# A mixture of softmaxes on one core: a unit of work takes every second row of a block of 256

## Chip, cores, metric

One core of a Trainium2 chip, the other cores idle. The metric is the device time of one execution in microseconds (us), as a median of several executions. Names in capitals are the core's engines: DVE (VectorE), ACT (ScalarE), POOL (GpSimd), SP (the engine that here only issues transfers).

## The reference

```python
# logits: (32, 128, 4, 4096) float32; prior: (32, 128, 4) float32
prior_probs = softmax(prior, axis=-1)
mixture = sum over the 4 heads of prior_probs[..., None] * softmax(logits, axis=-1)
# result: (32, 128, 4096) float32
```

268.4 MB of logits are read and 67.1 MB of result are written. A row (one batch and sequence position) has 4 heads of 4,096 floats, 64 KB that lie together in memory; its result is 16 KB.

## The kernel before

A unit of work is one batch: 128 rows, one per partition. It has 32 units, two logits buffers of 64 KB per partition, two result buffers, and two buffers for exponentials. Cut to what matters:

```python
P = 128                                   # B, S, H, V = 32, 128, 4, 4096

def load(b, eng=nc.sync):                 # issued from SP
    lt = lpool.tile([P, H, V], FP32, name="ltile")          # 2 buffers
    n = pieces(b)                         # 1 head at a time for the first unit and the last three, else all 4
    for h in range(0, H, n):
        eng.dma_start(out=lt[:, h : h + n], in_=logits[b, :, h : h + n, :])
    ltiles[b] = lt

def store(b, lo=0, hi=V, eng=nc.sync):    # issued from ACT in mid-run
    eng.dma_start(out=out[b, :, lo:hi], in_=accs[b][:, lo:hi])

# the prior: 32 partitions (batches) x 128 positions x 4 heads, softmax over heads,
# then turned by four 32-row transposes into pp[position, head, batch]
# ...
for b in range(B):
    # ... result tile acc; the store of unit b-1 is issued here
    for h in range(H):
        et = ebuf[:, h % 2]               # the last two units work in place
        nc.scalar.activation(et, lt[:, h], AF.Exp, accum_out=dsum[:, col])
        nc.vector.reciprocal(rden[:, col], dsum[:, col])
        if h == 0:
            nc.vector.tensor_scalar(out=acc, in0=et, scalar1=rden[:, col],
                                    scalar2=pp[:, h, b : b + 1], op0=ALU.mult, op1=ALU.mult)
            continue
        nc.gpsimd.tensor_mul(coeff[:, col], rden[:, col], pp[:, h, b : b + 1])
        nc.vector.scalar_tensor_tensor(out=acc, in0=et, scalar=coeff[:, col], in1=acc,
                                       op0=ALU.mult, op1=ALU.add)      # cut: the last head in two halves
    if b + 2 < B:
        load(b + 2)                       # waits until unit b has been read out of its buffer
```

The softmax here doesn't subtract the row's maximum and nothing guards it: scores larger than these inputs give would overflow.

## Time and profile before

| | before |
|---|---|
| time, median | 783.3 us (783.27 to 783.39, 6 runs) |
| span of the profiled run | 781.3 us |
| DVE busy, ACT busy | 68%, 60% |
| packets of the two data queues, share of 16 DMA engines' span | 82.1% + 17.6% |
| rate in mid-run | 433 GB/s |

The first lines are from the page of the kernel before: the span, the two data queues (packets, MB, share of the 16 DMA engines' time), the chain of waits that ended last (by engine and by line), and two groups of instructions (busy time, mean of one in ns, idle time before them and what ended most of it).

```profile
span 781.3 us, 851 instructions
...
q1 hardware_dynamic: 7056, 276.83, 82.1%
q10 hardware_dynamic: 4080, 58.79, 17.6%
...
DMA 66%; ACT 14%; DVE 10%; issue 7%; SPq 0%; POOL 0%; DVEq 0%; POOLq 0%; ACTq 0%
DMA ltile<-in_logits_dram 66%; ACT ebuf L107 14%; DVE acc L128 9%; DVE ltile L128 1%; SPq L43 0%; POOL coeff L123 0%; DVE rden L116 0%; DVEq L166 0%; DVE ltile L118 0%; POOLq L166 0%; ACTq L107 0%
...
L107 ACT ACTIVATE ebuf<-ltile 128x4096 f32<-128x4096 f32 x120 | 433.0, 3609 | 284.5 <-DMA ltile<-in_logits_dram 241.0
L116 DVE RECIPROCAL rden<-dsum 128x1 f32<-128x1 f32 x128 | 20.4, 160 | 206.3 <-ACT ebuf L107 206.3
...
```

The two queues together keep 16 DMA engines busy for 99.7% of the span. ACT and DVE have idle time, and what ends it is the arrival of logits (241.0 us on ACT) or the exponentials that follow from it (206.3 us on DVE). The chain of waits is two thirds logits loads.

The next lines are windows of the same trace: from and to, the length, the busy time of each engine, the granted clock, the share of the 16 DMA engines that was busy, and the rate in GB/s. Later windows are shown without the heading; their columns are these.

```profile
core 0: us, DVE busy (x) ACT busy (x) POOL busy (x), PEclk, DMA share, GB/s
100.00:200.00 100.00, 68.48 (x33) 60.68 (x34) 2.30 (x12) 1.00 1.00 433
200.00:300.00 100.00, 68.37 (x35) 61.27 (x33) 2.49 (x13) 1.00 1.00 433
300.00:400.00 100.00, 67.93 (x35) 59.38 (x34) 2.49 (x13) 1.00 1.00 433
```

Share 1.00 with 433 GB/s is 27.1 GB/s for each busy engine. Reading a rate and a share together is what most of this document does: a full share says only that packets were in flight, and the rate beside it says how long each took (a share of 0.99 went with only 278 GB/s in move_sbuf, experiment 4).

The trace also has a record of each DMA packet, with its size and duration. A logits row is one packet of 65,536 bytes in mid-run. The least of the 3,584 durations of such packets is 2,418 ns, and so are the median and the 95th percentile. A 16 KB packet takes 611 ns, whether it loads from HBM or stores to HBM. I call the time above these minimums (and those of the few smaller packets), summed over all packets of the two data queues and divided by 16 engines, the *slow-packet time* of a run: 2.2 us in the kernel before. The sum of the minimum times is 777.2 us per engine. The rest of the span, after a sixteenth of the time of all packets is taken off, is the time in which an engine had no packet: 1.7 us.

Last, the start of the run in order of time (start, duration, engine, line, operation; in brackets the idle time before and what ended it):

```profile
5.80 0.67 DVE L58 TENSOR_REDUCE pmax<-pr 32x128 f32<-32x512 f32 x1 [5.80 <-DMA pr<-in_prior_dram]
...
10.65 1.25 DVE L75 STREAM_TRANSPOSE pp<-pn 32x128 f32<-32x128 f32 x4
...
12.81 2.41 DVE L118 TENSOR_SCALAR acc<-ebuf,rden,pp 128x4096 f32<-128x4096 f32 x1
...
17.97 4.49 DVE L128 SCALAR_TENSOR_TENSOR acc<-ebuf,coeff,acc 128x4096 f32<-128x4096 f32 x1 [0.31 <-POOL coeff L123]
...
32.35 0.37 ACTq L49 DMA_DIRECT2D out_dram<-acc  x1
45.37 3.62 ACT L107 ACTIVATE ebuf<-ltile 128x4096 f32<-128x4096 f32 x1 [18.04 <-DMA ltile<-in_logits_dram]
```

The prior is ready at 11.9 us (last transpose), the first unit's first DVE pass starts at 12.81, its result is stored from 32.35 on, and load 1 has arrived at 45.37.

### The profile page before, as it was taken

How to read it: one execution, taken by the hardware profiler on the slowest of the kernel's cores; microseconds unless marked ns; L12 is line 12 of the kernel's file. 1: busy time of each engine (PE TensorE's matmuls, PEld its weight loads, DVE VectorE, ACT ScalarE, POOL GpSimd, SP SyncE). 2: the span in 40 equal slices, each digit the busy share in tenths (PEclk: the TensorE clock that was granted, in tenths of full speed). 3: DMA queues.
4: the chain of work that ended last, by engine and by line, in shares of the span. 5: the costliest groups of instructions: out<-in, count | busy, mean ns of one | idle time of the engine just before them, and what ended most of it. 6: DMA issues, size and time to landing. Idle time of an engine off the chain costs nothing.

```text
span 781.3 us, 851 instructions
## 1 busy us (share of the span) xinstructions
DVE 527.9 (68%) x266; ACT 470.0 (60%) x258; POOL 18.6 (2%) x100
## 2 busy tenths in 40 slices
DVE  4647677666786666865668666677666776668994
ACT  5366556755567555575555765547655577558971
POOL 0000000000000000000000000000000000000000
DMA  9999999999999999999999999999999999999998
GB/s 373 448 416 440 434 416 456 410 463 405 460 409 456 416 443 429 419 454 415 458 408 450 419 464 406 456 427 430 432 430 439 426 446 412 457 408 430 429 429 364
DMA packets 11143, 335.67 MB, mean 430 GB/s; under 512 B 1248, under 2 KB 1248, under 8 KB 1280
## 3 DMA queue, kind: packets, MB, share of 16 engines
q1 hardware_dynamic: 7056, 276.83, 82.1%
q10 hardware_dynamic: 4080, 58.79, 17.6%
q14 instruction: 7, 0.06, 0.0%
HBM read 268.50 MB, written 67.11 MB: 430 GB/s over the span
## 4 chain that ended last, share of the span: by engine, by line
DMA 66%; ACT 14%; DVE 10%; issue 7%; SPq 0%; POOL 0%; DVEq 0%; POOLq 0%; ACTq 0%
DMA ltile<-in_logits_dram 66%; ACT ebuf L107 14%; DVE acc L128 9%; DVE ltile L128 1%; SPq L43 0%; POOL coeff L123 0%; DVE rden L116 0%; DVEq L166 0%; DVE ltile L118 0%; POOLq L166 0%; ACTq L107 0%
## 5 line engine op out<-in xcount | busy, mean ns | idle before, releaser
L107 ACT ACTIVATE ebuf<-ltile 128x4096 f32<-128x4096 f32 x120 | 433.0, 3609 | 284.5 <-DMA ltile<-in_logits_dram 241.0
L128 DVE SCALAR_TENSOR_TENSOR acc<-ebuf,coeff,acc 128x4096 f32<-128x4096 f32 x90 | 403.6, 4484 | 27.4 <-POOL coeff L123 27.4
L116 DVE RECIPROCAL rden<-dsum 128x1 f32<-128x1 f32 x128 | 20.4, 160 | 206.3 <-ACT ebuf L107 206.3
L118 DVE TENSOR_SCALAR acc<-ebuf,rden,pp 128x4096 f32<-128x4096 f32 x30 | 72.4, 2412 | 1.3 <-DVE rden L116 0.3
L123 POOL TENSOR_TENSOR coeff<-rden,pp 128x1 f32<-128x1 f32 x96 | 18.4, 191 | 748.1 <-DVE rden L116 748.1
L107 ACT ACTIVATE ltile<-ltile 128x4096 f32<-128x4096 f32 x8 | 28.9, 3608 | 4.3 <-DMA ltile<-in_logits_dram 4.3
L128 DVE SCALAR_TENSOR_TENSOR ltile<-ltile,coeff 128x4096 f32<-128x4096 f32 (+1 forms) x7 | 27.0, 3874 | 1.8 <-POOL coeff L123 1.8
L107 ACT ACTIVATION_READ_ACCUMULATOR ebuf<-ltile 128x1 f32 x120 | 22.4, 187 | 0.0
L118 DVE TENSOR_SCALAR ltile<-ltile,rden,pp 128x4096 f32<-128x4096 f32 x2 | 4.8, 2412 | 0.1
L58 DVE TENSOR_REDUCE pmax<-pr 32x128 f32<-32x512 f32 x1 | 0.7, 674 | 5.8 <-DMA pr<-in_prior_dram 5.8
L62 ACT ACTIVATE pe<-pc 32x512 f32<-32x512 f32 x1 | 0.6, 628 | 4.8 <-DVE pc L60 4.8
L62 ACT ACT_TABLE_LOAD x1 | 1.3, 1283 | 1.2 <-PEq L155 1.2
L107 ACT ACTIVATION_READ_ACCUMULATOR ltile<-ltile 128x1 f32 x8 | 1.5, 186 | 0.0
L75 DVE STREAM_TRANSPOSE pp<-pn 32x128 f32<-32x128 f32 x4 | 1.2, 302 | 0.1
L64 DVE TENSOR_REDUCE psum<-pe 32x128 f32<-32x512 f32 x1 | 0.7, 674 | 0.7 <-ACT pe L62 0.7
L69 DVE TENSOR_TENSOR pn<-pe,prec 32x512 f32<-32x512 f32 x1 | 1.0, 1042 | 0.0
L66 DVE RECIPROCAL prec<-psum 32x128 f32<-32x128 f32 x1 | 0.9, 941 | 0.0
L60 DVE TENSOR_TENSOR pc<-pr,pmax 32x512 f32<-32x512 f32 x1 | 0.7, 680 | 0.0
L155 POOL MEMSET const-float32-0.0<- 128x1 f32 x1 | 0.1, 99 | 0.2 <-issue 0.2
L155 POOL MEMSET const-bfloat16-1.0<- 128x1 bf16 x1 | 0.1, 102 | 0.0
L155 POOL MEMSET const-uint8-127<- 128x1 uint8 x1 | 0.1, 102 | 0.0
L155 POOL MEMSET const-float32-1.0<- 128x1 f32 x1 | 0.1, 99 | 0.0
## 6 DMA issues: line engine op xcount, KB each, us to landing
out_dram<-acc ACTq DMA_DIRECT2D x28, 2048.0 KB, 29.3
ltile<-in_logits_dram SPq DMA_DIRECT2D x16, 2048.0 KB, 20.5
out_dram<-acc SPq DMA_DIRECT2D x2, 2048.0 KB, 32.9
out_dram<-ltile SPq DMA_DIRECT2D x1, 2048.0 KB, 21.2
out_dram<-ltile SPq DMA_DIRECT2D x2, 1024.0 KB, 8.7
ltile<-in_logits_dram SPq DMA_DIRECT2D x28, 32.3
pr<-in_prior_dram ACTq DMA_DIRECT2D x1, 64.0 KB, 5.0
```

The source lines that it names most:

```text
L58: nc.vector.reduce_max(pmax, pr, axis=AX.X)
L60: nc.vector.tensor_sub(pc, pr, pmax.unsqueeze(2).to_broadcast([B, S, H]))
L62: nc.scalar.activation(pe, pc, AF.Exp)
L64: nc.vector.reduce_sum(psum, pe, axis=AX.X)
L66: nc.vector.reciprocal(prec, psum)
L69: nc.vector.tensor_mul(pn.rearrange("b h s -> b s h"), pe, prec.unsqueeze(2).to_broadcast([B, S, H]))
L75: nc.vector.transpose(pp[32 * t : 32 * (t + 1)], pn[:, :, 32 * t : 32 * (t + 1)])
L107: ex = nc.scalar.activation(et, lt[:, h], AF.Exp, accum_out=dsum[:, col])
L116: nc.vector.reciprocal(rden[:, col], dsum[:, col])
L118: nc.vector.tensor_scalar(out=acc, in0=et, scalar1=rden[:, col], scalar2=pp[:, h, b : b + 1], op0=ALU.mult, op1=ALU.mult,)
L123: nc.gpsimd.tensor_mul(coeff[:, col], rden[:, col], pp[:, h, b : b + 1])
L128: nc.vector.scalar_tensor_tensor(out=acc[:, cs], in0=et[:, cs], scalar=coeff[:, col], in1=acc[:, cs], op0=ALU.mult, op1=ALU.add,)
```

## The change

A unit takes every second row of a block of 256 rows. The two units of a block read the even and the odd rows. What it was meant to gain is presumably better service from HBM. The prior's softmax has to follow the new order and works on 16 partitions of 256 positions instead of 32 of 128.

```diff
-    assert S == P and B == 32
+    J = 2
+    R = P * J
+    G = B * S // R
+    B = G * J
+    lg = logits.rearrange("b s h v -> (b s) h v").rearrange("(g p j) h v -> g j p h v", p=P, j=J)
+    ov = out.rearrange("b s v -> (b s) v").rearrange("(g p j) v -> g j p v", p=P, j=J)
+    pv = prior.rearrange("b s h -> (b s) h").rearrange("(g r) h -> g r h", r=R)
 # load and store:
-            eng.dma_start(out=lt[:, h : h + n], in_=logits[b, :, h : h + n, :])
+            eng.dma_start(out=lt[:, h : h + n], in_=lg[b // J, b % J, :, h : h + n, :])
-        eng.dma_start(out=out[b, :, lo:hi], in_=accs[b][:, lo:hi])
+        eng.dma_start(out=ov[b // J, b % J, :, lo:hi], in_=accs[b][:, lo:hi])
 # the prior (cut: softmax now in place, in pr and pmax):
-    pr = cpool.tile([B, S, H], FP32, name="pr")
+    pr = cpool.tile([G, R, H], FP32, name="pr")
+    pn = cpool.tile([32, H, R], FP32, name="pn")
+    nc.gpsimd.memset(pn, 0.0)
+    pq = pn.rearrange("g h (p j) -> g j h p", j=J)
-    pp = cpool.tile([P, H, B], FP32, name="pp")
-    for t in range(S // 32):
-        nc.vector.transpose(pp[32 * t : 32 * (t + 1)], pn[:, :, 32 * t : 32 * (t + 1)])
+    pp = cpool.tile([P, J, H, 32], FP32, name="pp")
+    for t in range(P // 32):
+        nc.vector.transpose(pp[32 * t : 32 * (t + 1)], pq[:, :, :, 32 * t : 32 * (t + 1)])
 # and pp[:, h, b : b + 1] becomes pp[:, b % J, h, b // J : b // J + 1]
```

By *pitch* I mean the distance in HBM between the rows of neighbouring partitions. The change doubles it: 128 KB instead of 64 KB for reads, 32 KB instead of 16 KB for writes.

More of the change, by code (lines that the diff above doesn't have):

```diff
@@ L26 @@
     P = 128
-    assert S == P and B == 32
+    J = 2
+    R = P * J
+    G = B * S // R
+    B = G * J
+    assert G * R == B * S and G <= 32
+    lg = logits.rearrange("b s h v -> (b s) h v").rearrange("(g p j) h v -> g j p h v", p=P, j=J)
+    ov = out.rearrange("b s v -> (b s) v").rearrange("(g p j) v -> g j p v", p=P, j=J)
+    pv = prior.rearrange("b s h -> (b s) h").rearrange("(g r) h -> g r h", r=R)
     lpool = ctx.enter_context(tc.tile_pool(name="lpool", bufs=2))
@@ L48, in store @@
     def store(b, lo=0, hi=V, eng=nc.sync):
-        eng.dma_start(out=out[b, :, lo:hi], in_=accs[b][:, lo:hi])
+        eng.dma_start(out=ov[b // J, b % J, :, lo:hi], in_=accs[b][:, lo:hi])
     load(0, eng=nc.sync)
-    pr = cpool.tile([B, S, H], FP32, name="pr")
-    nc.scalar.dma_start(out=pr, in_=prior)
+    pr = cpool.tile([G, R, H], FP32, name="pr")
+    nc.scalar.dma_start(out=pr, in_=pv)
     load(1, eng=nc.sync)
-    pmax = cpool.tile([B, S], FP32, name="pmax")
+    pn = cpool.tile([32, H, R], FP32, name="pn")
+    nc.gpsimd.memset(pn, 0.0)
+    pmax = cpool.tile([G, R], FP32, name="pmax")
     nc.vector.reduce_max(pmax, pr, axis=AX.X)
-    pc = cpool.tile([B, S, H], FP32, name="pc")
-    nc.vector.tensor_sub(pc, pr, pmax.unsqueeze(2).to_broadcast([B, S, H]))
-    pe = cpool.tile([B, S, H], FP32, name="pe")
-    nc.scalar.activation(pe, pc, AF.Exp)
-    psum = cpool.tile([B, S], FP32, name="psum")
-    nc.vector.reduce_sum(psum, pe, axis=AX.X)
-    prec = cpool.tile([B, S], FP32, name="prec")
-    nc.vector.reciprocal(prec, psum)
-    pn = cpool.tile([B, H, S], FP32, name="pn")
+    nc.vector.tensor_sub(pr, pr, pmax.unsqueeze(2).to_broadcast([G, R, H]))
+    nc.scalar.activation(pr, pr, AF.Exp)
+    nc.vector.reduce_sum(pmax, pr, axis=AX.X)
+    nc.vector.reciprocal(pmax, pmax)
     nc.vector.tensor_mul(
-        pn.rearrange("b h s -> b s h"), pe, prec.unsqueeze(2).to_broadcast([B, S, H])
+        pn[0:G].rearrange("g h r -> g r h"), pr, pmax.unsqueeze(2).to_broadcast([G, R, H])
     )
-    pp = cpool.tile([P, H, B], FP32, name="pp")
-    for t in range(S // 32):
-        nc.vector.transpose(
-            pp[32 * t : 32 * (t + 1)], pn[:, :, 32 * t : 32 * (t + 1)]
-        )
+    pq = pn.rearrange("g h (p j) -> g j h p", j=J)
+    pp = cpool.tile([P, J, H, 32], FP32, name="pp")
+    for t in range(P // 32):
+        nc.vector.transpose(pp[32 * t : 32 * (t + 1)], pq[:, :, :, 32 * t : 32 * (t + 1)])
     NCHUNK = 2
@@ L118 @@
                 nc.vector.tensor_scalar(
-                    out=acc, in0=et, scalar1=rden[:, col], scalar2=pp[:, h, b : b + 1],
+                    out=acc, in0=et, scalar1=rden[:, col], scalar2=pp[:, b % J, h, b // J : b // J + 1],
                     op0=ALU.mult, op1=ALU.mult,
@@ L122 @@
                 continue
-            nc.gpsimd.tensor_mul(coeff[:, col], rden[:, col], pp[:, h, b : b + 1])
+            nc.gpsimd.tensor_mul(coeff[:, col], rden[:, col], pp[:, b % J, h, b // J : b // J + 1])
             n = NCHUNK if split else 1
```

## The prediction

> **What bounds the kernel now.** The DMA engines, at their own rate. The queue table gives 82.1% + 17.6% = 99.7% of 16 engines' span to the two data queues. DVE is 68% busy and ACT 60%. In steady state (windows of one pair of units, 100 to 293 us) a unit of 10.49 MB takes 24.15 us: 434 GB/s, DMA share 1.00. The chain of waits repeats: 32.3 us of a logits load, two softmax heads, one DVE pass, the next load. ACT idles for loads 241 us over 32 waits.
>
> The DMA records show what limits that rate. A logits row moves as one 65,536-byte packet, and from the 5th to the 95th percentile it takes exactly 2,418 ns: 27.1 GB/s per engine, 434 GB/s for 16. A 16 KB store packet takes 611 ns. Packets that took longer than this minimum add up to 2.2 us per engine over the whole run, 1.8 us of it in the first 80 us. So the distance between their reads isn't what holds the engines. [...]
>
> **What the change does.** Bytes, transfers and the order on their queues stay: a row is still 64 KB contiguous. Only addresses change: partition p takes row 2p+j, so read pitch goes from 64 to 128 KB and write pitch from 16 to 32 KB.
>
> The prior's preparation now works on 16 partitions with twice the elements in each. From today's times (674 + 680 + 628 + 674 + 941 + 1042 + 4 x 302 ns, about 6 us) I estimate 10 to 12 us; a POOL fill runs beside the prior's load. It starts when the prior lands (5.8 us) and so ends near 17 us instead of 11.9; the first DVE pass then starts 4 to 5 us later than 12.8 us. Waits absorb most of it, so the first unit's last pass ends 1 to 2 us late, at about 34 us. Load 1 is in flight until 45 us, so the engines stay fed: off the critical path.
>
> **Worth.** At the packet minimum the transfers need 777 us per engine of a span of 781.3 us. All that a better address pattern could remove is the 2.2 us of slow packets, 0.3%. A gain of 2% (16 us) isn't there. A loss is possible if the new pitch makes engines collide in HBM. [...]
>
> **Predicted:** 783.4 us, 8 times in 10 between 781.0 and 788.0. Faster by over 2%: 0.01; within 2%: 0.93; slower by over 2%: 0.06.
>
> **What would show it.** Right: median 64 KB packet still 2,418 ns, DMA share 1.00 and 434 GB/s in mid-run windows, a unit every 24.15 us, the chain still two thirds logits loads; DVE prior operations about twice as long; the second load lands near 45 us. Wrong: packets longer than 2,418 ns[...], or shorter (then it was the reads and not the engines that set 2,418 ns); or an engine gap near 30 us because the first unit frees its buffer late.
>
> **What would make it wrong.** That 2,418 ns is an HBM figure of the 64 KB pitch and not the engine's own; [...] or that the head's slow packets grow.

The sum came to 783.4 us, the time before (783.3 us) with nothing taken away and nothing added: 777 us of packets at their minimum, 2.2 us of slow packets and about 2 us of other time make the span of 781.3 us. That engines might collide in HBM is a guess.

## The result

| | before | after |
|---|---|---|
| time, median (6 runs each) | 783.33 us | 783.49 us |
| range | 783.27 to 783.39 | 783.32 to 783.61 |
| 64 KB packet, median and 95th percentile | 2,418 and 2,418 ns | 2,418 and 2,418 ns |
| slow-packet time per engine | 2.2 us | 1.9 us |

The ratio of after to before is 1.0002, with a 95% interval from 0.9989 to 1.0015. Here and below a ratio is the mean time of one kernel's fast runs over that of the other's fast runs of the same rounds, so it is not quite the ratio of the medians. The result is correct. The time did not move.

The page after:

```profile
span 781.4 us, 853 instructions
...
q1 hardware_dynamic: 7056, 276.83, 82.1%
q10 hardware_dynamic: 4064, 58.79, 17.6%
...
DMA 66%; ACT 14%; DVE 10%; issue 7%; SPq 0%; POOL 0%; DVEq 0%; POOLq 0%; ACTq 0%
DMA ltile<-in_logits_dram 66%; ACT ebuf L110 14%; DVE acc L131 9%; DVE ltile L131 1%; SPq L51 0%; POOL coeff L126 0%; DVE rden L119 0%; DVEq L169 0%; DVE ltile L121 0%; POOLq L169 0%; ACTq L110 0%
...
L110 ACT ACTIVATE ebuf<-ltile 128x4096 f32<-128x4096 f32 x120 | 433.0, 3609 | 284.1 <-DMA ltile<-in_logits_dram 240.5
L119 DVE RECIPROCAL rden<-dsum 128x1 f32<-128x1 f32 x128 | 20.4, 159 | 203.8 <-ACT ebuf L110 203.8
...
```

The shares of the queues and of the chain are the same, and so are ACT's waits for logits (240.5 us against 241.0). The windows after:

```profile
100.00:200.00 100.00, 67.94 (x33) 60.16 (x34) 2.28 (x12) 1.00 1.00 433
200.00:300.00 100.00, 68.41 (x35) 61.30 (x33) 2.46 (x13) 1.00 1.00 433
300.00:400.00 100.00, 68.36 (x35) 59.35 (x34) 2.46 (x13) 1.00 1.00 433
```

And the start:

```profile
4.84 1.21 DVE L68 TENSOR_REDUCE pmax<-pr 16x256 f32<-16x1024 f32 x1 [4.84 <-DMA pr<-in_prior_dram]
...
13.45 1.78 DVE L80 STREAM_TRANSPOSE pp<-pn 32x256 f32<-32x256 f32 x4
15.27 2.41 DVE L121 TENSOR_SCALAR acc<-ebuf,rden,pp 128x4096 f32<-128x4096 f32 x1
...
18.06 4.49 DVE L131 SCALAR_TENSOR_TENSOR acc<-ebuf,coeff,acc 128x4096 f32<-128x4096 f32 x1 [0.31 <-POOL coeff L126]
...
32.30 0.37 ACTq L57 DMA_DIRECT2D out_dram<-acc  x1
44.84 3.62 ACT L110 ACTIVATE ebuf<-ltile 128x4096 f32<-128x4096 f32 x1 [17.87 <-DMA ltile<-in_logits_dram]
```

The prior's preparation got longer: 10.4 us (4.84 to 15.23) against 6.1 us (5.80 to 11.90). The prior landed 1.0 us earlier, so the first DVE pass is 2.5 us late (15.27 against 12.81). Already at the second pass only 0.1 us of that is left, because DVE had been idle for about 2.6 us between the two in the kernel before. The first store leaves at 32.30, earlier than before by 0.05 us.

### The profile page after: what moved, and what is told of

Same layout as the page of the kernel before. It is cut to its first block, busy times and chain, and to the rows that moved or that the text cites. A ratio compares the mean times of both kernels' runs of the same rounds, so it can differ in the third digit from the quotient of the medians.

```text
span 781.4 us, 853 instructions
## 1 busy us (share of the span) xinstructions
DVE 531.3 (68%) x266; ACT 470.4 (60%) x258; POOL 19.3 (2%) x101
## 3 DMA queue, kind: packets, MB, share of 16 engines
q10 hardware_dynamic: 4064, 58.79, 17.6%
## 4 chain that ended last, share of the span: by engine, by line
DMA 66%; ACT 14%; DVE 10%; issue 7%; SPq 0%; POOL 0%; DVEq 0%; POOLq 0%; ACTq 0%
DMA ltile<-in_logits_dram 66%; ACT ebuf L110 14%; DVE acc L131 9%; DVE ltile L131 1%; SPq L51 0%; POOL coeff L126 0%; DVE rden L119 0%; DVEq L169 0%; DVE ltile L121 0%; POOLq L169 0%; ACTq L110 0%
## 5 line engine op out<-in xcount | busy, mean ns | idle before, releaser
L110 ACT ACTIVATE ebuf<-ltile 128x4096 f32<-128x4096 f32 x120 | 433.0, 3609 | 284.1 <-DMA ltile<-in_logits_dram 240.5
L68 DVE TENSOR_REDUCE pmax<-pr 16x256 f32<-16x1024 f32 x1 | 1.2, 1207 | 4.8 <-DMA pr<-in_prior_dram 4.8
L73 DVE TENSOR_TENSOR pn<-pr,pmax 16x1024 f32<-16x1024 f32 x1 | 1.9, 1906 | 0.1
L71 DVE TENSOR_REDUCE pmax<-pr 16x256 f32<-16x1024 f32 x1 | 1.2, 1207 | 1.1 <-ACT pr L70 1.1
L80 DVE STREAM_TRANSPOSE pp<-pn 32x256 f32<-32x256 f32 x4 | 1.7, 434 | 0.1
L72 DVE RECIPROCAL pmax<-pmax 16x256 f32<-16x256 f32 x1 | 1.7, 1741 | 0.0
```

The source lines that it names most:

```text
L68: nc.vector.reduce_max(pmax, pr, axis=AX.X)
L71: nc.vector.reduce_sum(pmax, pr, axis=AX.X)
L72: nc.vector.reciprocal(pmax, pmax)
L73: nc.vector.tensor_mul(pn[0:G].rearrange("g h r -> g r h"), pr, pmax.unsqueeze(2).to_broadcast([G, R, H]))
L80: nc.vector.transpose(pp[32 * t : 32 * (t + 1)], pq[:, :, :, 32 * t : 32 * (t + 1)])
L110: ex = nc.scalar.activation(et, lt[:, h], AF.Exp, accum_out=dsum[:, col])
```

## The experiments

The result agrees with the prediction, so the question is whether it does for the stated reason. The theories:

- **A**: each DMA engine, or the way through which it alone reaches memory, moves 27.1 GB/s and no more. HBM has enough left, so addresses don't matter; the prior's preparation is hidden.
- **B**: the new pitch did gain something, and the heavier preparation of the prior took it back.
- **C**: HBM, or something else that all engines share, gives 434 GB/s in all, at either pitch.

There are 12 runs, in three groups on a chip each, all timed in 3 rounds beside the kernel before. Kernels that move data only, or mix up rows, give a wrong result.

### 1. The change without its addresses: rows_in_order

```diff
 # in the changed kernel
-    lg = ....rearrange("(g p j) h v -> g j p h v", p=P, j=J)
+    lg = ....rearrange("(g j p) h v -> g j p h v", p=P, j=J)      # out and pq likewise
```

> The changed kernel with everything of the change but its addresses: a unit takes 128 rows in order again (pitch 64 KB), while the prior keeps its 16-partition preparation. Theory A (the engines' own rate binds, the rest is hidden): 783.4 us, within 0.2% of before; 64 KB packets at 2,418 ns; load 1 lands near 45 us. Theory B (the pitch gained something and the heavier preparation ate it up, so that the sum is zero): slower than before by the preparation's cost, 2 to 4 us (0.3 to 0.5%). Theory C (HBM binds, at the same rate in both patterns): 783.4 us as well; this run does not tell A from C.

Measured: correct, 783.53 us against 783.29, ratio 1.0003 (0.9986 to 1.0020). Load 1 was there at 44.76 us.

### 2. The addresses alone: addresses_only

```diff
 # in the kernel before
-            eng.dma_start(out=lt[:, h : h + n], in_=logits[b, :, h : h + n, :])
+            eng.dma_start(out=lt[:, h : h + n], in_=lg[b // J, b % J, :, h : h + n, :])   # J = 2; stores likewise
```

> The kernel before with only the addresses of loads and stores changed (every second row of 256); the prior stays as before, so the coefficients belong to other rows and the result is wrong on purpose. Theory A: 783.4 us, within 0.2% of before, 64 KB packets at 2,418 ns. Theory B: faster than before by 2 to 4 us (0.3 to 0.5%). Theory C: 783.4 us.

Measured: wrong, 783.30 us against 783.29, ratio 1.0000 (0.9985 to 1.0015); slow-packet time 1.8 us. With run 1 this settles B: each half of the change by itself leaves the time as it was, within 0.2%. There were not two effects that cancelled.

### 3. Larger pitches: pitch_2mb, pitch_512k, addr_pitch_2mb, addr_pitch_512k

The first two take every 32nd or every 8th row, load the prior in that layout (`pr[p, g, j, h]`, no transposes) and give the right result. The last two are addresses_only with another J:

```diff
-    J = 2
+    J = 32        # or 8
```

> Each partition takes every 32nd row: read pitch 2 MB, write pitch 512 KB, 64 KB rows; the prior is loaded in that layout, no transposes; right result. Theory A: as long as HBM keeps up, 783.4 us and 2,418 ns; if this pitch, 16 times that of the change, makes engines collide, packets get longer and the time grows in proportion[...]. Theory C (HBM binds already at 64 KB pitch): packets change with the pitch at once, also at 128 KB, so a longer packet here and none at 128 KB speaks against it.

> As pitch_2mb, but every 8th row of 1024: read pitch 512 KB, write pitch 128 KB; right result. It asks where between 128 KB and 2 MB the packets begin to grow. [...] 783.4 us within 0.3%, under 3 us of slow packets per engine. If the loss grows with the pitch instead of setting in late: 786 to 795 us.

> addresses_only with every 8th row of 1024 (read pitch 512 KB, write pitch 128 KB) and the prior as before, so the result is wrong on purpose. pitch_512k changed the prior's load too (it landed at 22.8 us instead of 5.8) and scattered from 785 to 807 us; this run has the pitch alone. If the pitch does it: 785 to 807 us again and 64 KB packets over 2,418 ns. If the late prior did it: 783.4 us within 0.2%.

> addresses_only with every 32nd row (read pitch 2 MB, write pitch 512 KB), the prior as before, wrong on purpose. If the pitch cost pitch_2mb its 3.5%: 806 to 815 us again, slow packets of about 20 us per engine, nearly all of them loads. If its other prior did: 783.4 us.

| run | read pitch | time, median | before, same rounds | ratio (95% interval) | slow-packet time |
|---|---|---|---|---|---|
| before | 64 KB | 783.3 us | | | 2.2 us |
| addresses_only | 128 KB | 783.30 us | 783.29 us | 1.0000 (0.9985 to 1.0015) | 1.8 us |
| addr_pitch_512k | 512 KB | 786.08 us | 783.40 us | 1.0039 (1.0024 to 1.0054) | 3.6 us |
| addr_pitch_2mb | 2 MB | 807.62 us | 783.40 us | 1.0314 (1.0287 to 1.0340) | 19.7 us |
| pitch_512k | 512 KB | 785.5 and 787.3 us (fast), 801.7 and 807.4 us (slow) | 783.33 us | 1.0040 (1.0020 to 1.0060), fast runs | 3.6 us |
| pitch_2mb | 2 MB | 810.71 us | 783.29 us | 1.0354 (1.0322 to 1.0386) | 21.9 us |

So distance can matter, and the kernel before was not at a point where it does. The windows of addr_pitch_2mb:

```profile
0.00:50.00 50.00, 21.74 (x17) 16.76 (x10) 0.78 (x7) 1.00 0.95 372
100.00:200.00 100.00, 65.36 (x32) 58.91 (x33) 2.30 (x12) 1.00 1.00 426
200.00:300.00 100.00, 65.38 (x33) 59.53 (x35) 2.30 (x12) 1.00 1.00 426
760.00:803.00 43.00, 28.62 (x14) 19.51 (x12) 0.96 (x5) 1.00 0.88 360
```

In mid-run the engines are as busy as ever (share 1.00), but the rate is 426 instead of 433 GB/s: some packets are longer. Most 64 KB packets still take the minimum: the median is 2,418 ns as before, the upper quartile 2,493 ns and the 95th percentile 2,744 ns; one in three took over 2,425 ns. The stores of mid-run, at 512 KB pitch, stay fast: their packets add less than 0.1 us to the slow-packet time. The sum agrees with the time: 17.6 us more slow-packet time than before, and 4.6 us more in which an engine had no packet (6.3 us against 1.7), most of it at the end, where the engines finish apart. That makes 22.2 us, and the span grew by 22.2 us (803.5 against 781.3).

One expectation was off: the fast runs of pitch_512k lie 0.4% above the kernel before, with 3.6 us of slow packets, just over the 0.3% and 3 us expected. That engines collide in HBM at a large pitch is not shown; the longer packets and the lower rate are.

pitch_512k was a flawed experiment. Its prior came in 512 packets of 128 bytes between the logits and landed at 22.8 us, so more than the pitch had changed. Two of its four runs count as slow; the runs of the kernel before between them did not vary. With the pitch alone, addr_pitch_512k stays between 785.87 and 787.89 us. What made those two runs slow was not followed up.

C is hurt here but not dead. If HBM set the pace at 64 KB, I would expect any change of pattern to show (an assumption, not shown), and 64 to 128 KB does not (783.30 us against 783.29). But a shared limit outside HBM's addresses would look the same.

### 4. Logits out of SBUF: move_sbuf

Movement only: the 32 loads copy from a constant tile in SBUF, in the same packets.

```diff
-            eng.dma_start(out=lt[:, h : h + n], in_=logits[b, :, h : h + n, :])
+            eng.dma_start(out=lt[:, h : h + n], in_=src[:, h : h + n])
```

> Movement only: no softmax, the 32 loads of 8.39 MB come out of SBUF instead of HBM in the same packets (64 KB and 16 KB), the 32 stores of 2.1 MB go to HBM as before; the result is wrong on purpose. Theory A: 64 KB packets at 2,418 ns again, the same 27.1 GB/s without HBM on the read side, so about 777 us of packets per engine and 780 to 790 us in all, the fill of the source tile at the start included. Theory C (HBM reads set 2,418 ns): packets clearly other than 2,418 ns, shorter if SBUF answers faster. A third possibility, D: [...] packets become longer, which would leave A against C open.

Measured: 1,158 us, 64 KB packets of 3,522 to 4,066 ns, median 3,771.

```profile
100.00:500.00 400.00, 0.00 (x0) 1.78 (x9) 0.00 (x0) 1.00 1.00 325
500.00:1100.00 600.00, 0.00 (x0) 3.75 (x19) 0.00 (x0) 1.00 0.99 278
```

All engines are busy, at 278 GB/s in the second stretch. This is possibility D of the expectation: without HBM on the read side packets got longer, not shorter (3,771 ns in the median against 2,418). So a packet that stays within SBUF can be the slower one, but A and C are not told apart.

### 5. Movement without compute: move_all

Loads and stores of the kernel before and no softmax; stores send a constant tile. Two more things differ: the prior is not loaded, and every store leaves from ACT as soon as its unit's load has landed.

> Movement only, 64 KB pitch: the loads, packets and queues of the kernel before, but no softmax; the stores send a constant tile, so the result is wrong on purpose. Theory A (the engines' rate binds, compute is hidden): 778 to 785 us, as long as with the compute. Rival (the third of the chain of waits that is ACT and DVE is really paid): clearly shorter, by up to a quarter.

Measured: 791.5 us against 783.3, ratio 1.0106 (1.0091 to 1.0121). That is outside what theory A expected, on the side nobody expected: without any compute it is slower. The rival, that ACT's and DVE's third of the chain is paid, is refuted. The excess is in two places (the last line is the end of the kernel before):

```profile
20.00:100.00 80.00, 0.00 (x0) 0.59 (x3) 0.00 (x0) 1.00 1.02 437
200.00:300.00 100.00, 0.00 (x0) 0.59 (x3) 0.00 (x0) 1.00 1.02 435
770.00:789.00 19.00, 0.00 (x0) 0.20 (x1) 0.00 (x0) 1.00 0.65 276
...
770.00:781.00 11.00, 1.54 (x1) 0.00 (x0) 0.00 (x0) 1.00 0.78 332
```

With nothing to pace them, the stores pile up behind the loads (65 us from issue to landing in the median, against 29 us before), and at the end the engines finish unevenly: the last 19 us have a share of 0.65. Per engine, 6.3 us without a packet against 1.7, and 6.2 us of slow packets against 2.2: 8.6 us together, and the span grew by 8.3 (the prior's packets are missing here). Since the order of the stores changed too, this run alone is no exact bound. But in the kernel before an engine has no packet for only 1.7 us, so a faster ACT or DVE could bring back that much at most. It also shows that 777.2 us of packets per engine is a floor which not every order of issue comes close to.

### 6. Fewer engines: move_11_engines, ports_apart, ports_shared

move_11_engines is move_all on 88 of the 128 rows:

```diff
-            eng.dma_start(out=lt[:, h : h + n], in_=lg[b // J, b % J, :, h : h + n, :])
+            eng.dma_start(out=lt[0:88, h : h + n], in_=lg[b // J, b % J, 0:88, h : h + n, :])   # stores likewise
```

> As move_all, but every load and store takes 88 of the 128 rows. [...] So 11/16 of the bytes on 11/16 of the engines. Theory A (27.1 GB/s is each engine's own): packets stay at 2,418 ns, the time stays that of move_all within 1%, the rate falls to about 298 GB/s. Theory C (HBM or another shared resource gives 434 GB/s in all): packets shrink to about 2,418 x 11/16 = 1,660 ns and the time to about 540 us. The result is wrong on purpose.

Measured: 1,326 us; 64 KB packets of 4,794 ns in the median, 5,459 at most.

```profile
100.00:500.00 400.00, 0.00 (x0) 1.58 (x8) 0.00 (x0) 1.00 0.69 203
500.00:1200.00 700.00, 0.00 (x0) 3.36 (x17) 0.00 (x0) 1.00 0.69 151
```

A share of 0.69 is 11 of 16 engines busy on average, for 88 of 128 rows. But neither theory gave packets of about twice the length, and 31% fewer bytes than move_all took 68% more time. What I had not thought of is that it may matter which partitions of SBUF are written at the same time. The next two kernels test this alone. Each load is four transfers of 8 rows, the windows of both show a share of 0.49 to 0.52, which is 8 of 16 engines busy on average, and both kernels read the same rows from HBM:

```diff
 # ports_apart                                      # ports_shared
     for c in range(4):
-        ... out=lt[c : 32 : 4], in_=rows c : 32 : 4
+        ... out=lt[8 * c : 8 * c + 8], in_=rows c : 32 : 4
```

> Movement only, a quarter of the rows (32 of 128 of each unit) and one store at the end; wrong on purpose. Each load is four transfers of 8 rows[...]; here a transfer writes every fourth SBUF partition of 0 to 31[...]. Theory A1[...]: packets 2,418 ns, 217 GB/s, about 310 us in all. Theory A2 (the DMA engine itself moves 27.1 GB/s): the same. Theory C (HBM gives 434 GB/s in all): packets well under 2,418 ns, down to 1,209.

> As ports_apart, with the same rows read from HBM by the same number of engines, but each transfer writes 8 neighbouring partitions[...]. A2 (engine): 2,418 ns and about 310 us, as ports_apart. C: as ports_apart.

A1 is that SBUF's side of a transfer sets the pace, in a way that depends on which partitions are written together; A2 is the engine itself.

In both kernels the one store was issued at 5.16 us and not at the end, so in both it ran beside the first loads.

ports_apart: 323.0 us (322.93 to 323.08; about 310 were expected), 64 KB packets of 2,418 ns in the median, 2,458 at the 95th percentile.

```profile
20.00:70.00 50.00, 0.00 (x0) 0.98 (x5) 0.00 (x0) 1.00 0.50 215
120.00:170.00 50.00, 0.00 (x0) 0.99 (x5) 0.00 (x0) 1.00 0.51 220
220.00:270.00 50.00, 0.00 (x0) 0.99 (x5) 0.00 (x0) 1.00 0.49 212
```

Half the engines busy, about half the rate, the same packet. This is what refutes C: whatever all engines share was asked for 215 GB/s instead of 433, and packets did not get shorter (2,418 ns in the median). 27.1 GB/s belongs to the single engine, its way into SBUF, or its own way to HBM.

ports_shared: 452 to 503 us in four runs; three of them lie over 1.5% above the fastest and so count as slow, at the same granted clock, so only its packets and its distance from ports_apart (about 40% at the least) are used. The windows are of the profiled run, one of the slow ones (484.69 us):

```profile
20.00:70.00 50.00, 0.00 (x0) 1.68 (x3) 0.00 (x0) 1.00 0.52 95
120.00:170.00 50.00, 0.00 (x0) 0.59 (x3) 0.00 (x0) 1.00 0.50 136
220.00:270.00 50.00, 0.00 (x0) 0.59 (x3) 0.00 (x0) 1.00 0.50 127
370.00:420.00 50.00, 0.00 (x0) 0.99 (x5) 0.00 (x0) 1.00 0.51 206
```

The share is the same and the rate is not: 95 GB/s at first, up to 206 later. The first 16 packets took 7.5 to 9.1 us, 3.1 to 3.8 times the 2,418 ns of ports_apart. Over the whole run the median was 3,008 ns. A2 alone, which gave 2,418 ns, does not account for that, so A1 is possible. That writing to neighbouring partitions lengthens packets is shown; why it does, and why packets got shorter again in the course of the run, is not. Whether this explains the doubling in move_11_engines is open: only 5 of its 2,464 packets of 64 KB took under 2,500 ns, so all 11 engines were slowed, and how the rows were dealt to them was not looked at. Nor can these runs say whether, where nothing lengthens packets, it is the engine (A2), its way into SBUF (A1) or its own way to HBM that sets 2,418 ns: no run varied one of these alone and got shorter packets, and move_sbuf, which could have excluded HBM, had longer packets (3,771 ns) instead.

### 7. How much delay the start hides: slack_30

```diff
+    for _ in range(16):
+        nc.vector.tensor_mul(pn[0:G].rearrange("g h r -> g r h"), pr, pmax...)    # 1.9 us each
     nc.vector.tensor_mul(pn[0:G].rearrange("g h r -> g r h"), pr, pmax...)
```

> The changed kernel with the last operation of the prior's preparation done 16 more times, 1.9 us each: 30.5 us of delay before the first DVE pass, right result. Theory A, with the slack that I read: the first unit hides about 13 us of delay (load 2 may be issued at any time until load 1's packets end near 43 us; today it is issued near 28 us). With 30.5 us I expect load 2 to be issued near 57 us, a gap in the DMA of 13 to 16 us, and 796 to 800 us in all. If nothing of it were hidden: 814 us; if all of it: 783.5 us.

Measured: correct, 801.04 us against 783.33, ratio 1.0227 (1.0210 to 1.0244). The windows, then the lines that explain them:

```profile
20.00:40.00 20.00, 19.66 (x12) 0.00 (x0) 0.00 (x0) 1.00 1.08 466
42.00:57.00 15.00, 14.44 (x10) 7.42 (x4) 0.38 (x2) 1.00 0.00 0
100.00:200.00 100.00, 68.75 (x35) 60.68 (x34) 2.46 (x13) 1.00 1.00 434
```

```profile
46.12 2.41 DVE L125 TENSOR_SCALAR acc<-ebuf,rden,pp 128x4096 f32<-128x4096 f32 x1
48.57 3.62 ACT L114 ACTIVATE ebuf<-ltile 128x4096 f32<-128x4096 f32 x1 [31.52 <-DVE acc L125]
...
56.91 0.33 SPq L51 DMA_DIRECT2D ltile<-in_logits_dram  x1
```

Load 2 was issued at 56.91 us, as expected (27.00 us in the changed kernel). The packet records show no data packet for 15.8 us, from about 42 to 58 us; the expectation was a gap of 13 to 16. Against the changed kernel there are also 0.9 us more of slow packets and 1.0 us more of other time without a packet. That makes 17.7 us, and the span grew by 17.8 us (799.2 against 781.4); the median time grew by 17.6, to 1 us above the 796 to 800 us that I had expected. So of 30.5 us of delay about 13 were free. The 2.5 us that the change brought lie far inside.

## Why the prediction was right, point by point

- *The DMA engines' own rate binds.* Confirmed. Packets of 2,418 ns with 16 engines busy and with 8 (ports_apart, share 0.50); no time below 783 us without compute (move_all, 791.5 us). The prediction spoke of the engine; the runs leave open whether it is the engine, its way into SBUF or its own way to HBM. On SBUF's side, ports_shared shows that writing to neighbouring partitions cost time (452 us at the least against 323.0).
- *Bytes and transfers stay, only addresses change; at most 0.3% is to be had.* Confirmed: slow-packet time 2.2 us before, 1.9 after, 1.8 with the addresses alone. There was no slow reading of HBM for the change to repair.
- *A loss is possible if the new pitch makes engines collide in HBM.* There was none at 128 KB (783.30 us against 783.29). Larger pitches cost time: 0.4% at 512 KB, and 3.1% at 2 MB, where the rate in mid-run fell by about 2% (433 to 426 GB/s). So in these runs a loss was there at 512 KB and not yet at 128 KB. Whether engines collide is not shown.
- *The prior takes 10 to 12 us and the first DVE pass starts 4 to 5 us late.* The first holds at its lower end (10.4 us), the second is too large: 2.5 us. Three terms were off. I took the transposes as twice as long (604 ns each), and they took 434; the other operations took 1.8 times as long and not twice (8.3 us in all instead of 9.3); and I took the prior's arrival as unchanged, and it came 1.0 us earlier.
- *The first unit's last pass ends 1 to 2 us late.* Too large: the store after it left 0.05 us earlier than before. I had not set the delay against the 2.6 us or so for which DVE is idle before its second pass.
- *Off the critical path.* Confirmed, with its limit: about 13 us of delay at the start are free (slack_30).

## What to carry to other kernels

Before changing an access pattern, look for the cost that it would remove: divide the rate by the busy share and look at whether packets exceed their minimum. If they all take the minimum, there is no slow packet that another order of addresses could repair. But the minimum has to be one that other runs reach too: in move_sbuf even the fastest 64 KB packet took 3,522 ns. A full DMA share does not say whether the limit is shared or each engine's own; a transfer on half of the engines does (ports_apart: share 0.50, 215 GB/s, packets still 2,418 ns), if nothing else lengthens its packets, as writing to neighbouring partitions did in ports_shared (share 0.52, 95 GB/s).
